# Block 0's residual added after the sums, its squares turned through DRAM, and another pair of PSUM banks, in a decoder trunk with emulated fp32

## The chip, the cores and the metric

The kernel runs on one core of a Trainium2 chip. TensorE does the matmuls and transposes, VectorE and ScalarE the elementwise work, GpSimd (POOL in the profile) and SyncE (SP) issue most DMAs. The metric is the device time of one execution in microseconds. Three runs of the kernel before took 2192.23, 2192.76 and 2198.56 us; the median is 2192.76.

## The reference

One sequence of 256 rows and 2048 features passes through two layers. Layer 0 mixes with gated linear attention, layer 1 with block attention over a shared K/V; each is followed by a gated convolutional FFN, and each part adds its output to the residual h. Cut to what the change touches:

```python
def gla_mixer(x, ...):
    ...
    return o.reshape(B, S, GLA_VAL_DIM).astype(x.dtype) @ w_out

def conv_ffn(x, norm_w, w_up, conv_w, conv_b, w_down):
    h = rms_norm(x, norm_w) @ w_up
    ...
    return (jax.nn.silu(a) * u) @ w_down

def reference(...):
    for layer in range(DEPTH):
        h = h + gla_mixer(...)          # layer 0; moba_mixer in layer 1
        h = h + conv_ffn(h, ffn_norm[layer], ...)
    return h
```

All inputs are float32. Four matrix products end in a residual add: the output projections of the two mixers ("go" and "mo", 2048 by 2048) and the down projections of the two FFNs ("dn0" and "dn1", 5632 by 2048).

## The kernel before

Each float32 operand of a product is split in a high part and the rest (`whi`, `wlo` for weights), and three products of parts are summed in PSUM. For weights, ScalarE casts the high part (L140) and VectorE subtracts it (L141); both run a few steps ahead of TensorE. Weight chunks of 1 MB come by SyncE's queue into `wraw`. One matmul instruction is 128x128 by 128x512.

go, dn0, mo and dn1 all go through `down`. It makes the output in two blocks of 1024 features, b = 0 and 1. A block is a 2 by 2 arrangement of 128x512 pieces: two halves of the rows (t) and two halves of the features (f). Some contraction steps use seven products in place of eight, with sums of operands (`comb`, and weight sums t13 and t24 made by VectorE at L106 to L108); the others are plain. Products carry the numbers 1 to 8. Products 1 and 6, and 5 and 7, share a two-bank tile each and are used by seven-steps only. After the last seven-step they are evacuated: ScalarE copies product 1 into the SBUF tile c0 (L754), VectorE adds the others, giving four tiles c0 to c3 (L755 to L758), and GpSimd issues four accumulating DMAs that add the residual to them (L760). Products 2, 3, 4 and 8 go on. 2 and 3 share a two-bank tile (`low`, "acc" in the trace), 4 and 8 have a bank each ("p"). A block ends with a tail of plain steps, first for f = 0 (products 2 and 4), then for f = 1 (3 and 8); after each, VectorE adds the finished products onto c0 and c2, or c1 and c3 (L769), so it needs the accumulate to have landed, and the piece is done: `done` stores it to DRAM as rows (L782, "rows" in the trace) and ScalarE sums its squares for the next norm (L317). The next block takes new tiles from the same pools, and its first matmuls into a tile wait for the last read of what was there.

The next GEMM needs the sums with features on the partitions. `back` makes that from row pieces: four TensorE transposes (L793) of 128x128, then `make_xw` (ScalarE L253, VectorE L255) scales and splits them into `xw`. `TURNS` says in which block and after which tail step of go and mo the first six of the eight `back` calls come; entry (1, (0, 1)) means block 1, f = 0, step 1. The other two follow the second block.

`turned` holds another way to turn rows into features, used elsewhere in the kernel: VectorE transposes 32x32 squares into `z` (`square`, L384), GpSimd stores z to DRAM (`store`, L387) and loads it back as four strided DMAs (`load`, L393). `through` schedules store, load and the jobs that use the result.

The order on each engine is the order in which the program issues instructions. `after(n, job)` runs a job n weight steps later; `ws.behind()` places what is issued inside it behind the latest weight cast and subtraction. Engines run their queues in order and wait on semaphores; GpSimd's DMAs all stand in one queue of instructions. The four stages lie at about 292 to 383 us (go), 863 to 1110 (dn0), 1381 to 1472 (mo) and 1960 to 2184 (dn1).

Of the kernel before, what the change touches and what calls it, by code (L numbers as in the profile page):

```python
# [9 lines left out]
F32R = mybir.dt.float32r  # L10
I32 = mybir.dt.int32
AF = mybir.ActivationFunctionType
OP = mybir.AluOpType
# [5 lines left out]
S = 256  # L19
KT = D // 128  # L20
NP = KT // 2
# [30 lines left out]
}  # L52


TURNS = ((0, (1, 2)), (0, (1, 2)), (1, (0, 1)), (1, (0, 1)), (1, (1, 2)), (1, (1, 2)))


class WeightStream:
# [99 lines left out]
def trunk(ctx: ExitStack, tc: tile.TileContext, xT, x_tok, cst, msk, w1p, w2a, w_k, w_qa, w_v2, w_v, w_g, w_go,  # L158
          w_up0, w_dn0, w_kk, w_kv, w_mq, w_mo, w_up1, w_dn1, rel, onehot, out):
    nc = tc.nc  # L160
    V, A, T = nc.vector, nc.scalar, nc.tensor
# [11 lines left out]
    def slot(shape, dt, name):  # L173
        return big.tile(shape, dt, name=name, tag="slot")

    def temp(name, shape=(128, 2, S), dt=F32):
        return tmp.tile(list(shape), dt, name=name, tag="temp")

    def bank(name, shape):
        return mis_ps.tile(list(shape), F32, name=name, tag="bank")  # L180
# [5 lines left out]
    ws = WeightStream(tc, raw, parts)  # L186
# [59 lines left out]
    def col(c):  # L246
        return gn[:, c - C_GN:c - C_GN + 1] if C_GN <= c < C_GN + KT else cs[:, c:c + 1]

    def make_xw(p, c, name, src):
        x = slot([128, 2, 2 * S], F32R, name)  # L250
        for i in range(2):
            n = col(c + 2 * p + i)
            hi = A.activation(x[:, i, :S], src[:, i, :], AF.Copy, scale=n)  # L253
            ws.first = ws.first or hi.ins
            V.scalar_tensor_tensor(x[:, i, S:], src[:, i, :], n, x[:, i, :S].bitcast(F32),  # L255
                                   op0=OP.mult, op1=OP.subtract)
        return x

    def spread_sum(ps, sq):
# [9 lines left out]
    def after(steps, job):  # L269
        later.append((cur[0] + steps, job))  # L270
# [31 lines left out]
    def split(dst_hi, dst_lo, src):  # L302
        A.copy(dst_hi, src)
        V.tensor_sub(dst_lo, src, dst_hi.bitcast(F32))

    class Norm:
# [9 lines left out]
        def square(self, t, c, src):  # L316
            A.activation(temp("junk", (128, 512)), src, AF.Square, accum_out=self.ss[:, t, c:c + 1])  # L317
# [27 lines left out]
    nrm = Norm(C_GN, "xw")  # L345
# [9 lines left out]
    xs = rows(nrm.xs)  # L355
# [187 lines left out]
    fresh, square, through = turned("keys", 2)  # L543
# [45 lines left out]
    for g in range(2):  # L589
        z = gemm_tok(xs, 1, lambda ps: evacuated(ps, col16))  # L590
        jobs = []
# [107 lines left out]
                after(7 + 2 * i, lambda J=J, i=i: convolve(2 * J + i, f[J][:, 2 * i:2 * i + 2, :]))  # L699
        then(hid, sums)  # L700

    def down(name, xs, combos, res, done, jobs):

        for b, (order, n_tail) in enumerate(ORDERS[name]):
            new = [k for k, seven in order if seven and k not in combos]
            todo = {i: list(js) for i, js in jobs.get(b, {}).items()}
            for k in new:
                at = next(i for i, (k_, _) in enumerate(order) if k_ == k)
                todo.setdefault(max(at - 2, 0), []).append(lambda k=k: combine_parts(k, xs, combos))
            low = acc_ps.tile([128, 2, 512], F32, name="acc")  # L710
            p = {2: low[:, 0], 3: low[:, 1], 4: bank("p4", (128, 512)), 8: bank("p8", (128, 512))}
            left = dict.fromkeys(range(1, 9), 0)
            for k, seven in order:
                for n in ((1, 5, 7, 6, 4, 3, 2) if seven else (2, 3, 4, 8, 2, 3, 4, 8)):
                    left[n] += 3
            begun = set()

            def prods(*todo):

                w = step()  # L720
                for n, _, _ in todo:
                    if n not in p:
                        two = acc_ps.tile([128, 2, 512], F32, name="acc")
                        p.update({n: two[:, 0], {1: 6, 5: 7}[n]: two[:, 1]})
                for xi, wi in ((0, 0), (1, 0), (0, 1)):
                    for n, x, f in todo:
                        left[n] -= 1
                        T.matmul(p[n], x[xi], w[wi][:, 512 * f:512 * f + 512], start=n not in begun, stop=left[n] == 0)  # L728
                        begun.add(n)

            def part(k, i, t):
                x = xs[k][:, i, 128 * t:]
                return x[:, :128], x[:, S:S + 128]

            def comb(k, f):
                return combos[k][:, f, 0], combos[k][:, f, 1]

            last = max(i for i, (k, seven) in enumerate(order) if seven)
            for i, (k, seven) in enumerate(order[:-n_tail]):
                for job in todo.get(i, ()):  # L740
                    job()
                if seven:
                    prods((1, part(k, 0, 0), 0))
                    prods((3, comb(k, 3), 0), (2, part(k, 1, 0), 1))
                    prods((5, comb(k, 0), 0), (7, comb(k, 2), 1))
                    prods((6, comb(k, 1), 0), (4, part(k, 1, 1), 1))
                else:
                    for a in range(2):
                        prods(*((n, part(k, a, t), f)
                                for n, t, f in ((2, 0, a), (3, 0, 1 - a), (4, 1, a), (8, 1, 1 - a))))  # L750
                if i == last:

                    r = [temp(f"c{n}", (128, 512)) for n in range(4)]
                    A.copy(r[0], p[1])  # L754
                    V.tensor_add(r[1], r[0], p[6])  # L755
                    V.tensor_add(r[2], r[1], p[7])
                    V.tensor_add(r[1], r[1], p[5])
                    V.tensor_add(r[3], r[2], p[5])  # L758
                    for n in (0, 2, 1, 3):
                        nc.gpsimd.dma_start(r[n], res(n // 2, 2 * b + n % 2), accum_op=OP.add)  # L760
            for f, ns in enumerate(((2, 4), (3, 8))):
                for i, (k, _) in enumerate(order[-n_tail:]):
                    for job in todo.get((f, i), ()):
                        job()
                    prods(*((n, part(k, a, t), a) for a in range(2) for t, n in enumerate(ns)))
                if f:
                    ws.prefetch(cur[0])
                for t, n in enumerate(ns):
                    V.tensor_add(r[2 * t + f], r[2 * t + f], p[n])  # L769
                    done(t, 2 * b + f, r[2 * t + f])  # L770

    def scratch(name):
        t = dram.tile([2, 128, D], F32, name=name)
# [37 lines left out]

    def middle(name, xs, combos, res, nrm, keep_row, at, feature_major, parked=None):
        done, back, in_acc, in_bank = onward(nrm, keep_row, parked)
        jobs = {}
        for q, (b, i) in enumerate(at):
            jobs.setdefault(b, {}).setdefault(i, []).append(lambda q=q: back(q, in_acc))
        down(name, xs, combos, res, done, jobs)
        for q in range(len(at), NP):
            after(1 if feature_major else q - 3, lambda q=q: back(q, in_bank))
        after(2 if feature_major else 3, nrm.close)  # L820
        if feature_major:
            after(3, nrm.weave)
# [169 lines left out]
    xs = rows(xkv)  # L992
# [125 lines left out]
```

## Time and profile before

| | before |
|---|---|
| median of three runs | 2192.76 us |
| profiled execution | 2190.33 us |
| its span | 2188.5 us |
| PE busy | 2169.5 us, 99% |
| DVE busy | 1594.4 us, 73% |
| ACT busy | 1283.9 us, 59% |
| POOL busy | 301.9 us, 14% |
| accumulating DMAs (L760), issue to landing | 4.1 to 10.4 us, median 8.8 |
| stores of rows (L782), issue to landing | 2.6 to 7.5 us, median 4.0 |

The span runs from the first to the last instruction; the profiled execution's own time is 1.8 us longer. PE is TensorE's matmuls and PEld its weight loads, which overlap; DVE is VectorE, ACT ScalarE. "p<-whi,hid" is an instruction that writes p and reads whi and hid. In a timeline row the bracket gives how long the engine was idle before it and what ended that.

### The profile page before, as it was taken

How to read it: one execution, taken by the hardware profiler on the slowest of the kernel's cores; microseconds unless marked ns; L12 is line 12 of the kernel's file. 1: busy time of each engine (PE TensorE's matmuls, PEld its weight loads, DVE VectorE, ACT ScalarE, POOL GpSimd, SP SyncE). 2: the span in 40 equal slices, each digit the busy share in tenths (PEclk: the TensorE clock that was granted, in tenths of full speed). 3: DMA queues.
4: the chain of work that ended last, by engine and by line, in shares of the span. 5: the costliest groups of instructions: out<-in, count | busy, mean ns of one | idle time of the engine just before them, and what ended most of it. 6: DMA issues, size and time to landing. Idle time of an engine off the chain costs nothing.

```text
span 2188.5 us, 26953 instructions
## 1 busy us (share of the span) xinstructions
PE 2169.5 (99%) x9693; PEld 1793.0 (82%) x9693; DVE 1594.4 (73%) x2190; ACT 1283.9 (59%) x1856; POOL 301.9 (14%) x448
## 2 busy tenths in 40 slices
PE   9999999999999999999999999999999999999999
PEld 7888887888888888778888888888888888887787
DVE  6655687667676767987867787776777676779886
ACT  6545665556565556555556676555656565656554
POOL 1011111111111111000013242011111111110000
PEclk9999999999999999999999999999999999999999
DMA  8466577677777777566577887676777777775655
GB/s 318 176 231 211 185 245 257 208 239 232 249 244 237 247 238 244 176 234 239 205 262 261 273 277 230 207 234 225 236 249 235 247 238 245 239 245 189 234 206 173
DMA packets 92248, 510.11 MB, mean 233 GB/s; under 512 B 13729, under 2 KB 14769, under 8 KB 42194
## 3 DMA queue, kind: packets, MB, share of 16 engines
q1 hardware_dynamic: 60722, 417.53, 54.4%
q0 software_dynamic: 30816, 90.28, 15.2%
q8 instruction: 76, 1.25, 0.2%
q10 hardware_dynamic: 576, 0.58, 0.1%
q14 instruction: 58, 0.48, 0.1%
HBM read 463.22 MB, written 45.11 MB: 232 GB/s over the span
## 4 chain that ended last, share of the span: by engine, by line
PE 88%; issue 9%; DMA 2%; ACT 1%; DVE 0%; POOL 0%; SPq 0%; DVEq 0%; ACTq 0%; POOLq 0%
PE acc L290 44%; PE acc L293 22%; PE acc L728 12%; PE p L728 7%; DMA c<-rows 1%; DMA w2s<-w2a 0%; PE sT L561 0%; PE o L578 0%; ACT whi L140 0%; PE acc L793 0%; DMA wraw<-w_v 0%; PE s L910 0%; POOL upT L667 0%; DMA gn<-cst 0%; PE z L428 0%
## 5 line engine op out<-in xcount | busy, mean ns | idle before, releaser
L141 DVE TENSOR_TENSOR wlo<-wraw,whi 128x1024 fp32r<-128x1024 f32 (+1 forms) x786 | 930.3, 1191 | 423.3 <-ACT whi L140 402.2
L140 ACT CAST whi<-wraw 128x1024 fp32r<-128x1024 f32 (+1 forms) x786 | 798.8, 1026 | 639.1 <-PE acc L290 417.9
L290 PE MATMUL acc<-whi,xw 128*128 128x512 f32 x3840 | 952.3, 390 | 2.4 <-ACT whi L140 1.7
L290 PEld LDWEIGHTS acc<-whi,xw 128*128 128x128 f32 x3840 | 719.6, 188 | 153.8 <-ACT whi L140 2.8
L293 PE MATMUL acc<-wlo,xw 128*128 128x512 f32 x1920 | 514.3, 389 | 0.0
L293 PEld LDWEIGHTS acc<-wlo,xw 128*128 128x128 f32 x1920 | 360.3, 188 | 74.6
L728 PE MATMUL acc<-whi,hid 128*128 128x512 f32 x572 | 182.3, 390 | 4.5 <-DVE c L769 3.8
L728 PE MATMUL p<-whi,hid 128*128 128x512 f32 x506 | 166.2, 390 | 0.0
L667 POOL DMA_DIRECT2D upT<-turned x176 | 114.3, 656 | 146.4 <-DMA turned<-z 59.3
L140 ACT CAST whi<-t 128x1024 fp32r<-128x1024 f32 x82 | 85.5, 1051 | 77.9 <-PE p L728 42.6
L728 PEld LDWEIGHTS acc<-whi,hid 128*128 128x128 f32 x572 | 106.8, 188 | 28.1 <-DVE c L769 4.6
L290 PE MATMUL acc<-whi,xkv 128*128 128x512 f32 x512 | 128.8, 391 | 0.0
L661 POOL DMA_DIRECT2D turned<-z x44 | 34.2, 776 | 678.1 <-DVE z L657 615.6
L676 ACT ACTIVATE au<-upT,cs 128x256 f32<-128x256 f32 x176 | 96.0, 595 | 45.4 <-DMA upT<-turned 45.3
L728 PE MATMUL acc<-whi,comb 128*128 128x512 f32 x328 | 108.0, 394 | 4.4 <-ACT whi L140 4.3
L728 PEld LDWEIGHTS p<-whi,hid 128*128 128x128 f32 x506 | 94.9, 188 | 19.8
L290 PEld LDWEIGHTS acc<-whi,xkv 128*128 128x128 f32 x512 | 94.6, 188 | 18.6
L141 DVE TENSOR_TENSOR wlo<-t,whi 128x1024 fp32r<-128x1024 f32 x82 | 99.1, 1220 | 4.8 <-ACT whi L140 3.5
L680 DVE SCALAR_TENSOR_TENSOR au<-upT,cs,au 128x255 f32<-128x255 f32 x176 | 77.4, 472 | 33.8 <-ACT au L676 33.7
L728 PE MATMUL acc<-wlo,hid 128*128 128x512 f32 x286 | 94.9, 391 | 1.4 <-DVE wlo L141 1.4
L760 POOL DMA_DIRECT2D c<-rows x24 | 21.2, 1052 | 465.2 <-DVE c L755 453.4
L728 PE MATMUL p<-wlo,hid 128*128 128x512 f32 x253 | 83.6, 389 | 0.0
(251 smaller groups left out, 1951.4 us busy)
## 6 DMA issues: line engine op xcount, KB each, us to landing
wraw<-w_up SPq DMA_DIRECT2D x176, 1024.0 KB, 5.3
wraw<-w_dn SPq DMA_DIRECT2D x88, 1024.0 KB, 4.9
turned<-z POOLq DMA_DIRECT2D x44, 512.0 KB, 3.5
upT<-turned POOLq DMA_DIRECT2D x176, 128.0 KB, 4.8
wraw<-w_g SPq DMA_DIRECT2D x16, 1024.0 KB, 4.9
wraw<-w_go SPq DMA_DIRECT2D x16, 1024.0 KB, 6.2
wraw<-w_mq SPq DMA_DIRECT2D x16, 1024.0 KB, 5.8
wraw<-w_kk SPq DMA_DIRECT2D x16, 1024.0 KB, 5.6
```

The lines of the kernel that those rows point to most:

```text
L140: one = nc.scalar.copy(hi[:, a:b], src[:, a:b])
L141: two = nc.vector.tensor_sub(lo[:, a:b], src[:, a:b], hi[:, a:b].bitcast(F32))
L290: T.matmul(ps[:, t, :], xs(kt)[:, x0 + 128 * t:x0 + 128 * t + 128], hi[:, c:c + 512], start=kt == 0 and x0 == 0, stop=False)
L293: T.matmul(ps[:, t, :], xs(kt)[:, 128 * t:128 * t + 128], lo[:, c:c + 512], start=False, stop=kt == KT - 1)
L661: nc.gpsimd.dma_start(turned[J].rearrange("(a i) r q c -> (i r) a (q c)", a=4), z.rearrange("p (a q) t c -> p a (q t c)", a=4))
L667: nc.gpsimd.dma_start(f[32 * q:32 * q + 32].rearrange("p a (i c) -> p (a i) c", i=4), turned[J][:, :, q, :].rearrange("a r c -> r a c"))
L676: A.activation(au[:, i, :], t[:, i, :], AF.Identity, bias=col(cb + n), scale=col(cw + 2 * 2 * FT + n))
L680: V.scalar_tensor_tensor(au[:, i, 1:], t[:, i, :S - 1], col(cw + 2 * FT + n), au[:, i, 1:], op0=OP.mult, op1=OP.add)
L728: T.matmul(p[n], x[xi], w[wi][:, 512 * f:512 * f + 512], start=n not in begun, stop=left[n] == 0)
L760: nc.gpsimd.dma_start(r[n], res(n // 2, 2 * b + n % 2), accum_op=OP.add)
```

## The change

Three edits, two of them for go and mo only.

In go and mo the first block's accumulating DMAs no longer follow the last seven-step. They are issued one by one after VectorE's add of each finished sum. Four weight steps later `to_dram` stores the rows, sums the squares, and VectorE turns the piece by 32x32 squares into a z tile shared by both row halves. When the second half is in, z goes through DRAM, and eight and nine steps after that `turned_xw` scales the loaded squares on ScalarE (four 128x128 activations each), casts and subtracts (`split`). The four `back` calls of block 0 go away with their transposes, and `TURNS` keeps two entries.

In dn0 and dn1 products 3 and 8 now share the two-bank tile, and 2 and 4 have a bank each. In go and mo the pair stays (2, 3).

```diff
-TURNS = ((0, (1, 2)), (0, (1, 2)), (1, (0, 1)), (1, (0, 1)), (1, (1, 2)), (1, (1, 2)))
+TURNS = ((1, (1, 2)), (1, (1, 2)))
...
+    def turned_xw(p, c, name, f):
+
+        x, w = slot([128, 2, 2 * S], F32R, name), temp("w")
+        for i in range(2):
+            for t in range(2):
+                A.activation(w[:, i, 128 * t:128 * t + 128].rearrange("p (t i c) -> p t i c", t=2, i=2),
+                             f[:, i, :, t::2], AF.Copy, scale=col(c + 2 * p + i))
+        split(x[:, :, :S], x[:, :, S:], w)
+        return x
...
-            p = {2: low[:, 0], 3: low[:, 1], 4: bank("p4", (128, 512)), 8: bank("p8", (128, 512))}
+            pair, single = ((3, 8), (2, 4)) if name.startswith("dn") else ((2, 3), (4, 8))
+            p = {n: low[:, i] for i, n in enumerate(pair)}
+            p.update({n: bank(f"p{n}", (128, 512)) for n in single})
...
-                    for n in (0, 2, 1, 3):
-                        nc.gpsimd.dma_start(r[n], res(n // 2, 2 * b + n % 2), accum_op=OP.add)
+                    if b or not first_done:
+                        for n in (0, 2, 1, 3):
+                            nc.gpsimd.dma_start(r[n], res(n // 2, 2 * b + n % 2), accum_op=OP.add)
...
-                    V.tensor_add(r[2 * t + f], r[2 * t + f], p[n])
-                    done(t, 2 * b + f, r[2 * t + f])
+                    x = r[2 * t + f]
+                    V.tensor_add(x, x, p[n])
+                    if b or not first_done:
+                        done(t, 2 * b + f, x)
+                    else:
+                        nc.gpsimd.dma_start(x, res(t, f), accum_op=OP.add)
+                        after(4, lambda t=t, f=f, x=x: first_done(t, f, x))
...
+        fresh, square, through = turned(f"first_{name}", 2)
+        zs = []
+
+        def to_dram(t, c, x):
+            if t == 0:
+                zs.append(fresh())
+            with ws.behind():
+                done(t, c, x)
+                square(zs[c], x, t)
+            if t:
+                through(c, zs[c], [(8 + i, lambda f, i=i: nrm.xs.append(
+                    turned_xw(2 * c + i, nrm.c, nrm.name, f[:, 2 * i:2 * i + 2]))) for i in range(2)])
+
+        jobs, first = {}, 4 if feature_major else 0
...
-        down(name, xs, combos, res, done, jobs)
+        down(name, xs, combos, res, done, jobs, to_dram if feature_major else None)
```

`Norm.xs`, which `turned_xw` appends to, is the list of `xw` tiles that the next GEMM reads. Line numbers move: L728 becomes L740, L760 becomes L773 (the early accumulates) and L787 (those after the sums), L769 becomes L783, L782 L800, L384, L387 and L393 become L394, L397 and L403, and L317 L327.

TensorE in dn0, before: the end of block 0 and the start of block 1. acc_6975 holds products 2 and 3, p8_6977 product 8, acc_7917 is a tile of the next block.

```order
L728 MATMUL p8_6977<-whi_7811,hid_6943 128x512 [waits Activation_49]
L728 MATMUL p8_6977<-whi_7811,hid_6943 128x512 x3
L728 MATMUL p8_6977<-wlo_7812,hid_6943 128x512 [waits DVE_49]
L728 MATMUL p8_6977<-wlo_7812,hid_6943 128x512
L728 MATMUL p8_6977<-whi_7827,hid_7123 128x512 x4
L728 MATMUL p8_6977<-wlo_7828,hid_7123 128x512 x2
L728 MATMUL acc_7917<-whi_7853,hid_3445 128x512 [waits Activation_49]
L728 MATMUL acc_7917<-whi_7853,hid_3445 128x512 x3
L728 MATMUL acc_6975<-whi_7793,hid_6764 128x512 [waits DVE_49]
L728 MATMUL acc_6975<-whi_7793,hid_6764 128x512 x3
L728 MATMUL acc_6975<-wlo_7794,hid_6764 128x512 x2
```

The same place after the change, where acc_6989 holds products 3 and 8, and p2_7932 and p4_7933 belong to the next block:

```order
L740 MATMUL acc_6989<-wlo_7826,hid_6956 128x512 [waits DVE_49]
L740 MATMUL acc_6989<-wlo_7826,hid_6956 128x512 x3
L740 MATMUL acc_6989<-whi_7841,hid_7137 128x512 x8
L740 MATMUL acc_6989<-wlo_7842,hid_7137 128x512 x4
L740 MATMUL p2_7932<-whi_7867,hid_3458 128x512 [waits DVE_49,Activation_49]
L740 MATMUL acc_7931<-whi_7867,hid_3458 128x512 x2
L740 MATMUL p2_7932<-whi_7867,hid_3458 128x512
L740 MATMUL acc_7931<-whi_7867,hid_3458 128x512 x2
L740 MATMUL p2_7932<-wlo_7868,hid_3458 128x512 [waits DVE_49]
L740 MATMUL acc_7931<-wlo_7868,hid_3458 128x512
L740 MATMUL p4_7933<-whi_7867,hid_3458 128x512 [waits DVE_49]
```

The wait on DVE that stood before product 3's matmuls is no longer there; the first wait on DVE for a tile's last reader now stands at p2 of the next block, and the one at p4 comes after eight matmuls of that block.

GpSimd in go, block 0, before: accumulates of the residual (x_tok) into the c tiles, then stores of the finished rows.

```order
L760 DMA c0_2585<-x_tok 128x512 [waits DMASW1_49,DVE_49]
L760 DMA c1_2586<-x_tok 128x512 [waits DMASW2_49,DVE_49]
L760 DMA c2_2587<-x_tok 128x512 [waits DMASW3_49,DVE_49]
L760 DMA c3_2588<-x_tok 128x512
L782 DMA rows1_2415<-c0_2585 128x512 [waits DMASW5_49,DVE_49]
L782 DMA rows1_2415<-c2_2587 128x512 [waits DMASW6_49,DVE_49]
L782 DMA rows1_2415<-c3_2588 128x512 [waits DMASW7_49,DVE_49]
L782 DMA rows1_2415<-c1_2586 128x512 [waits DMASW0_49,DVE_49]
```

After the change, with the first store of z behind them:

```order
L787 DMA c0_2586<-x_tok 128x512 [waits DMASW1_49,DVE_49,Activation_49]
L787 DMA c2_2588<-x_tok 128x512 [waits DMASW2_49,DVE_49]
L800 DMA rows1_2415<-c0_2586 128x512 [waits DMASW3_49,DMASW1_49]
L787 DMA c3_2589<-x_tok 128x512 [waits DVE_49]
L800 DMA rows1_2415<-c2_2588 128x512 [waits DMASW5_49,DMASW2_49]
L800 DMA rows1_2415<-c3_2589 128x512 [waits DMASW6_49,DMASW4_49]
L787 DMA c1_2587<-x_tok 128x512 [waits DMASW7_49,DVE_49,Activation_49]
L800 DMA rows1_2415<-c1_2587 128x512 [waits DMASW7_49,DMASW0_49]
L397 DMA first_go_2420<-z_2782 128x1024 [waits DVE_49]
```

Each store of rows now waits for the accumulate that fills the tile which it stores, and the accumulates of c3 and c1 stand behind such stores in the queue.

VectorE in go after the change, where block 0's pieces c0 to c3 are turned into the z tiles (L394) between weight subtractions of block 1 (L141):

```order
L394 STREAM_TRANSPOSE z_2782<-c0_2586 128x4x4x32 [waits DMASW1_49]
L394 STREAM_TRANSPOSE z_2782<-c2_2588 128x4x4x32 [waits DMASW2_49]
L141 TENSOR_TENSOR wlo_2866<-t13_2736,whi_2865 128x1024 [waits PE_49]
L141 TENSOR_TENSOR wlo_2809<-t24_2660,whi_2808 128x1024 [waits Activation_49]
L141 TENSOR_TENSOR wlo_2892<-wraw_2722,whi_2891 128x1024 [waits DMAHW3_49,PE_49,Activation_49]
L141 TENSOR_TENSOR wlo_2919<-wraw_2761,whi_2918 128x1024 [waits DMAHW4_49,PE_49,Activation_49]
L394 STREAM_TRANSPOSE z_2845<-c1_2587 128x4x4x32 [waits DMASW7_49]
L394 STREAM_TRANSPOSE z_2845<-c3_2589 128x4x4x32 [waits DMASW4_49]
L141 TENSOR_TENSOR wlo_2855<-wraw_2684,whi_2854 128x1024 [waits Activation_49]
L141 TENSOR_TENSOR wlo_2949<-wraw_2858,whi_2948 128x1024 [waits DMAHW5_49,PE_49,Activation_49]
```

The DMASW waits of the L394 rows are those for the accumulates; the subtractions that follow stand behind them. In the order before, the last row that waits for an accumulate of block 0 is the L769 add of c1, ahead of all the subtractions shown here.

## Rows read from the trace of the kernel before

**Rows 1.** The page: busy time by engine, and the chain by engine.
```profile
PE 2169.5 (99%) x9693; PEld 1793.0 (82%) x9693; DVE 1594.4 (73%) x2190; ACT 1283.9 (59%) x1856; POOL 301.9 (14%) x448
...
PE 88%; issue 9%; DMA 2%; ACT 1%; DVE 0%; POOL 0%; SPq 0%; DVEq 0%; ACTq 0%; POOLq 0%
```
**Rows 2.** TensorE's waits, whole span: total us, times, longest.
```profile
PE acc L728 <- ACT whi L140: 5.1, 4, 2.9
PE acc L728 <- DVE c L769: 3.8, 2, 2.0
...
PE p L728 <- DVE wlo L141: 0.5, 1, 0.5
```
**Rows 3.** The chain of waits at 344 to 346 us: start, us, what.
```profile
344.58 0.45 PE acc L793 x4
```
**Rows 4.** Timeline of TensorE in dn0 between the blocks: start, us, instruction.
```profile
973.53 1.07 PE L728 MATMUL p<-whi,hid 128*128 128x512 f32 x4
...
977.61 1.07 PE L728 MATMUL acc<-whi,hid 128*128 128x512 f32 x4
980.64 1.19 PE L728 MATMUL acc<-whi,hid 128*128 128x512 f32 x4 [1.96 <-DVE c L769]
```
**Rows 5.** Timeline of VectorE at the same place.
```profile
979.89 0.69 DVE L769 TENSOR_TENSOR c<-c,acc 128x512 f32<-128x512 f32 x1 [7.57 <-DMA c<-rows]
980.50 2.35 DVE L141 TENSOR_TENSOR wlo<-wraw,whi 128x1024 fp32r<-128x1024 f32 x2
```
**Rows 6.** Line L760 in dn0's first block (968 to 976 us).
```profile
DMA to landing us min/median/max: 9.0/10.0/10.3
```
**Rows 7.** Timeline of TensorE in dn1 between the blocks.
```profile
2067.32 1.19 PE L728 MATMUL acc<-whi,hid 128*128 128x512 f32 x4 [1.84 <-DVE c L769]
```
**Rows 8.** Timeline of VectorE at the end of dn1.
```profile
2180.58 0.69 DVE L769 TENSOR_TENSOR c<-c,p 128x512 f32<-128x512 f32 x1 [1.86 <-PE p L728]
2184.66 0.69 DVE L769 TENSOR_TENSOR c<-c,acc 128x512 f32<-128x512 f32 x1 [3.39 <-PE acc L728]
```
**Rows 9.** Timeline of ScalarE in go, start of block 1.
```profile
345.01 0.62 ACT L140 CAST whi<-wraw 128x512 fp32r<-128x512 f32 x1 [4.42 <-PE acc L793]
...
347.52 1.04 ACT L140 CAST whi<-t 128x1024 fp32r<-128x1024 f32 x1 [1.52 <-DVE t L106]
348.47 1.04 ACT L140 CAST whi<-wraw 128x1024 fp32r<-128x1024 f32 x1
```
**Rows 10.** Timeline of TensorE in go.
```profile
328.69 0.39 PE L728 MATMUL p<-wlo,go 128*128 128x512 f32 x1
...
349.56 0.80 PE L728 MATMUL acc<-whi,comb 128*128 128x512 f32 x1 [2.93 <-ACT whi L140]
350.16 0.63 PE L728 MATMUL acc<-whi,go 128*128 128x512 f32 x1
350.58 0.63 PE L728 MATMUL acc<-whi,comb 128*128 128x512 f32 x1
...
352.65 0.40 PE L728 MATMUL p<-whi,go 128*128 128x512 f32 x1
```
**Rows 11.** Windows in go: stretch, us, busy by engine, PEclk, DMA share, GB/s.
```profile
340.00:360.00 20.00, 17.07 (x72) 13.67 (x71) 15.61 (x18) 11.70 (x15) 0.00 (x0) 0.91 0.59 221
```
**Rows 12.** Line L760 in go's first block (318 to 330 us).
```profile
DMA to landing us min/median/max: 4.2/6.1/9.0
```
**Rows 13.** Groups of ScalarE by form, L317: busy, mean ns, idle before.
```profile
L317 ACT ACTIVATE junk<-c 128x512 f32<-128x512 f32 x24 | 15.0, 626 | 28.9 <-DVE c L769 24.1 <-PE acc L793 4.8
L317 ACT ACTIVATION_READ_ACCUMULATOR junk<-c 128x1 f32 x24 | 4.5, 186 | 0.0
```
**Rows 14.** Line L387, the stores of turned squares, whole span.
```profile
DMA to landing us min/median/max: 2.6/3.2/10.2
```
**Rows 15.** Line L393, the loads of turned squares, whole span.
```profile
DMA to landing us min/median/max: 2.8/5.0/8.0
```
**Rows 16.** Timeline of TensorE in mo, the step after the f = 0 tail.
```profile
1419.03 1.07 PE L728 MATMUL p<-whi,ox 128*128 128x512 f32 x4
```
**Rows 17.** Line L760 in mo's first block (1405 to 1420 us).
```profile
DMA to landing us min/median/max: 8.4/9.5/10.1
```
**Rows 18.** Line L760 in mo's second block (1440 to 1470 us).
```profile
DMA to landing us min/median/max: 6.5/7.1/8.7
```

More of the change, by code (lines that the diff above doesn't have):

```diff
@@ L700, in ffn, with down @@
         then(hid, sums)
-    def down(name, xs, combos, res, done, jobs):
+    def down(name, xs, combos, res, done, jobs, first_done=None):
         for b, (order, n_tail) in enumerate(ORDERS[name]):
@@ L813, in middle @@
         done, back, in_acc, in_bank = onward(nrm, keep_row, parked)
-        jobs = {}
+        fresh, square, through = turned(f"first_{name}", 2)
[10 more added lines that the diff above has]
+        jobs, first = {}, 4 if feature_major else 0
         for q, (b, i) in enumerate(at):
-            jobs.setdefault(b, {}).setdefault(i, []).append(lambda q=q: back(q, in_acc))
-        down(name, xs, combos, res, done, jobs)
-        for q in range(len(at), NP):
+            jobs.setdefault(b, {}).setdefault(i, []).append(lambda q=q: back(first + q, in_acc))
+        down(name, xs, combos, res, done, jobs, to_dram if feature_major else None)
+        for q in range(first + len(at), NP):
             after(1 if feature_major else q - 3, lambda q=q: back(q, in_bank))
```

## The prediction

> **What bounds the kernel now.** I read the page first, then the waits of TensorE, then single engines around the four places that the diff touches. The page shows TensorE busy for 99% of the span and carrying 88% of the chain of waits [rows 1]. So time can come only from fewer TensorE instructions, or from TensorE's few waits. Those are short: the two largest groups in the list are four waits on ScalarE's casts, 5.1 us together with one of 2.9, and two waits on VectorE's add at L769, 3.8 us [rows 2]. A third thing to look for is new waits: VectorE and ScalarE have spare time, but their queues are in order, and the change puts waits for DMAs into them.
>
> **TensorE's instructions.** Four transposes take 0.45 us on the chain [rows 3], 0.1125 each. `TURNS` shrinks from six entries to two, so four of `back` go in each of go and mo, with four transposes each: 2 x 4 x 4 = 32 transposes, 32 x 0.1125 = **3.6 us less**. Matmuls are the same in number. All 32 stand on TensorE, so this term holds unless a wait eats it.
>
> **Down projections, between the blocks.** In dn0 the f = 0 tail ends and p8's last 18 matmuls begin at 973.53; 4 of the next block's follow at 977.61; then p3 waits until 980.64, 1.96 us [rows 4]. p3 shares a tile with p2, and p2's reader, VectorE's c0 add, began at 979.89 after 7.57 us of waiting for a DMA [rows 5], an accumulate that took 9.0 to 10.3 us to land [rows 6]. Afterwards p3 and p8 share the tile, both are unread, and their 36 matmuls run on: 36 x 0.227 = 8.2 us (the matmul step is that from 973.53 to 977.61: 18 in 4.08), so to 981.7. The new block's first product needs p2, whose add ends at 979.89 + 0.69 = 980.6: in time. Next late is p4: its add stands in VectorE's queue behind three wlo subtractions of about 1.17 each [rows 5], so it ends at 980.6 + 3.5 + 0.7 = 984.8, and TensorE is there after 8 more matmuls, at 983.5. The next block's products wait about 1.2 instead of 1.96: 0.8 less (0 to 1.96). In dn1 the wait is 1.84 [rows 7], and fewer subtractions stand between; I take 1.2 of it as gained (0 to 1.84). Together **2.0 less** (0 to 3.8).
>
> **The end of dn1.** Before, p8's add came at 2180.58 and only p3's, at 2184.66, after the last matmul [rows 8]. Now both adds read the tile that ends last: one add more in series, 2180.58's 0.69, less some overlap: **0.6 more** (0.5 to 0.7). The two stores leave on different queues.
>
> **go, the wait that is there.** ScalarE's cast at 345.01 waited 4.42 us because the L317 and L253 work before it waited for transposes; through VectorE's subtraction and L106 it made the casts of 347.52 and 348.47 late [rows 9]; TensorE stood still for 2.93 us until 349.56, and then issued matmuls 0.42 to 0.43 us apart (350.16, 350.58) instead of 0.23 [rows 10]: the granted clock, 0.91 over 340 to 360 [rows 11], had gone to its lower level, 1.2 GHz instead of 2.4, after the stand-still. Seven matmuls took 3.09 us (349.56 to 352.65) instead of 1.59. The place costs 2.93 + 1.5 = 4.4 us, and with the transposes gone this cause is gone.
>
> **go, the waits that come.** The first block's accumulates now start after its sums are finished, and the POOL order puts stores that wait for a landing between them: c0, c2, store of c0 (waits for c0's landing), c3, stores of c2 and c3 (wait for c3's landing), and only then c1. Three landings stand in series. The f = 0 tail ended at 328.69 + 0.23 [rows 10]; 6 matmuls now stand before its end, so 330.3; the add (0.69) and the issue make c0 start at about 331.3. Two store issues of 0.55 lie between, so c1 lands at 332.4 + 3L. The nearest row for L is go's first block itself: 4.2 to 9.0, median 6.1 [rows 12]. I take 6.1: c1 lands at 350.7.
> Behind it: on ScalarE the squares of c1 and c3 (0.63 each and a read of 0.19 [rows 13]), then four casts 0.95 apart [rows 9]; on VectorE two 32x32 transposes (estimated as other 128x512 operations there, 0.69), then wlo subtractions. Counting TensorE's order at 0.227 per matmul from 330.3, the subtraction behind the two transposes is needed at 353.6, and it ends 7.3 us after c1 lands: no wait while c1 lands before 346.3. At 350.7 TensorE waits 4.4, and a stand-still as long as the present one would again cost about 1.5 at the lower clock: 5.9 against 4.4 now, **1.5 more**. The bounds are L = 4.2 (c1 at 345.0, no wait, 4.4 less) and L = 8.0, short of the largest row since three in series will not all be the longest (356.4: 10.1 + 1.5, so 7.2 more). The store of the squares and its loads (L387 3.2, L393 5.0 median [rows 14, 15]) come after c1, but the 16 activations that read them stand far enough behind it: nothing.
> The Trainium skill, "DMA: Bandwidth & Descriptors", section "Anatomy of one DMA — SWDGE (gpsimd) path", gives such a DMA about 2.0 us plus its bytes over 436 GB/s, so an estimate of 2.6 us for 256 KB. The trace disagrees, with 4.2 at the least in go and 10.3 at the most in dn0 [rows 6, 12]; by the rule three in series would be 7.8 us, and the time would come out as in rival A.
>
> **mo.** Now TensorE loses 0.5 us there, on a subtraction [rows 2]. The f = 0 tail ends at 1419.03 [rows 16], so c0's accumulate would start at about 1420.0. Afterwards POOL's order is c0, c2, the stores of both, c3, c1: two landings in series. L is 8.4 to 10.1, median 9.5 [rows 17]: c2 is issued at 1421.0, lands at 1430.5; c1 is issued at 1432.1 and lands at 1441.6. The same squares and transposes stand before casts that TensorE needs from 1443.5 on; no wait before 1440.2, so 1.4 (0 to 2.6). Then c1's and c3's squares are stored and loaded back: 1441.6 + 0.7 for the transposes, 0.6 + 3.2 for the store, four issues of 0.55 and 5.0 for the loads make 1453.3; eight small activations and two casts (4 us, an estimate) stand before the copy that opens the second block's residual chain, at 1457.4. Its accumulates (6.5 to 8.7 [rows 18]) land about 1466.5, when by its order TensorE wants the banks: 1.5 (0 to 4). Less the 0.5 of now: **2.4 more** (0.5 less to 6 more).
>
> **Sum.** -3.6 - 2.0 + 0.6 + 1.5 + 2.4 = -1.1. The profiled execution took 2190.33 us; 2189.2. The median of the runs shown, 2192.76, lies 2.4 above it, so 2191.6.
>
> **Rivals.** *A, the accumulates land early* (chance 0.30). If L falls to 4.2 in go and 6.5 in mo, because fewer transfers are under way together than when four were issued in a row, no new wait arises: -3.6 - 2.0 + 0.6 - 4.4 - 0.5 = -9.9, so 2182.9. For it: go's shortest landings; ScalarE and VectorE are not full. Against it: every accumulate of dn0 took 9.0 or more [rows 6].
> *B, POOL's series of landings stalls the cast queues* (0.24). With L = 8 in go and 10.1 in mo: -3.6 - 2.0 + 0.6 + 7.2 + 6 = +8.2, so 2201.0. It decides from L of about 7.4 in go; mo's and the second blocks' landings speak for it, go's own median against.
> *C, nothing is gained in the down projections* (within the forecast): p2's or p4's adds still wait for the same DMAs, so the stall only moves to the next block's first products; 2.0 is lost and the time is 2193.6. For it: the landing of c2's accumulate, which I did not move.
> *D, the change does what it says but the order is not what sets it* (within the forecast): waits in the profile are small, so everything is hidden and 3.6 - 0.6 remain: 2189.8.
>
> **How the numbers follow.** The forecast with C and D has 0.46; A 0.30; B 0.24. A measurement of this kernel can't tell less than about 0.3%, 6.6 us, from no change. A lies 9.9 below, so most of it is faster; some of it falls within, and a little of the forecast below -6.6: faster 0.30. B gives slower 0.23. The range must hold 8 in 10: from A's end, 2182, to just past B's, 2201; the forecast's own range is 2186 to 2198.
>
> **What would show it.** Right: no TensorE wait on c L783 between the blocks of dn0 and dn1, or one of about 1 us on the add of p4; two adds after the last matmul; in go a TensorE wait of some 4 us between 350 and 358, with ScalarE's square L327 or VectorE's L394 waiting for DMA c<-x_tok before it; in mo waits of 1 to 2 us near 1445 and 1467. Wrong: no wait in go at all (A), or one of over 8 us followed by a low clock (B); 1.9 us still lost between the blocks of dn0 (C).

## The result: slower, and the profile after

The changed kernel took 2209.76 us (median, 2207.36 to 2215.76), against 2193.9 us (2191.66 to 2198.56) for the kernel before in the same runs: a ratio of 1.0073, with a 95% interval of 1.0062 to 1.0083. The prediction was 2191.6 us, with 2182 to 2201 as its range and 0.23 for slower. The time lies outside.

First the page, against [rows 1]: TensorE's busy time and instructions, then the chain.

```profile
PE 2172.8 (99%) x9661; PEld 1790.2 (81%) x9661; DVE 1596.2 (72%) x2190; ACT 1290.7 (59%) x1880; POOL 312.7 (14%) x468
...
PE 89%; DMA 4%; issue 3%; DVE 2%; ACT 1%; POOL 1%; SPq 0%; DVEq 0%; POOLq 0%; ACTq 0%
```

There are 9661 TensorE records in place of 9693: the 32 transposes are gone. The chain now has 4% DMA in place of 2%. The span is 2205.6 us instead of 2188.5. Here are TensorE's waits over the whole span (total, times, longest), which answer to [rows 2].

```profile
PE acc L740 <- ACT whi L140: 12.1, 6, 7.3
PE p L740 <- ACT whi L140: 4.4, 3, 3.0
PE p L740 <- DVE wlo L141: 3.6, 4, 1.1
PE acc L740 <- DVE wlo L141: 2.3, 8, 0.7
```

The matmuls' waits on the add of the sums (3.8 us) have left the list. Their waits on ScalarE's casts have grown from 5.1 to 16.5 us, and one of them lasts 7.3.

To see where, I split each trace at four instructions of TensorE: the first matmul that reads the operand of go, of dn0 (hid), of mo (ox) and of dn1 (hid). The last column runs to the last matmul. Each stretch holds the stage and what comes between it and the next.

| stretch | before | after | longer by |
|---|---|---|---|
| go, to the start of dn0 | 571.55 | 585.46 | 13.91 |
| dn0, to the start of mo | 517.81 | 517.33 | -0.48 |
| mo, to the start of dn1 | 570.81 | 573.39 | 2.57 |
| dn1, to the last matmul | 232.31 | 232.83 | 0.52 |

So 14 of 17 us are in go's row, and in go itself: the next GEMM's first matmul comes 105.4 us after go's first, where it came 91.4 after it. TensorE's timeline there (start, us, instruction, wait and releaser) answers to [rows 10]; the window below it answers to [rows 11].

```profile
349.87 1.46 PE L740 MATMUL acc<-whi,comb 128*128 128x512 f32 x5 [0.96 <-ACT whi L140]
...
358.10 0.73 PE L740 MATMUL p<-whi,go 128*128 128x512 f32 x2 [2.96 <-ACT whi L140]
...
372.90 0.79 PE L740 MATMUL acc<-whi,comb 128*128 128x512 f32 x1 [7.27 <-ACT whi L140]
373.49 0.63 PE L740 MATMUL p<-whi,go 128*128 128x512 f32 x1
373.92 0.63 PE L740 MATMUL acc<-whi,comb 128*128 128x512 f32 x1
```

```profile
360.00:380.00 20.00, 12.04 (x39) 8.64 (x38) 10.08 (x11) 8.60 (x16) 4.94 (x9) 0.77 0.59 185
```

Of the wait of 2.93 at 349.56, 0.96 is left at 349.87. New are 2.96 and 7.27; after the long one the matmuls come 0.43 us apart (373.49, 373.92) at the lower clock, 1.2 GHz, and the granted clock of the window is 0.77. Go back from 372.90: ScalarE's timeline, then VectorE's.

```profile
355.78 0.63 ACT L327 ACTIVATE junk<-c 128x512 f32<-128x512 f32 x1 [2.83 <-DMA c<-x_tok]
...
370.85 1.04 ACT L140 CAST whi<-wraw 128x1024 fp32r<-128x1024 f32 x1 [10.01 <-DMA wraw<-w_go]
```

```profile
361.06 1.30 DVE L394 STREAM_TRANSPOSE z<-c 128x512 f32<-128x512 f32 x2
362.29 1.18 DVE L141 TENSOR_TENSOR wlo<-wraw,whi 128x1024 fp32r<-128x1024 f32 x1
```

The wait of 2.96 is the one that the prediction was about: c1's accumulate lands, the square L327 of 355.78 starts, the cast behind it is late. The long one is not. ScalarE waited 10.01 us for a weight chunk, `wraw<-w_go`. SyncE issued its load only at 363.49, when the subtraction that ends at 362.29 + 1.18 = 363.47 had read the buffer's old chunk for the last time; the load took 7.3 us:

```profile
DMA to landing us min/median/max: 7.3/7.3/7.3
```

SyncE's load issues after (the row holds three from 352.06, the last at 375.5) and before (five from 337.98):

```profile
352.06 23.72 SPq L96 DMA_DIRECT2D wraw<-w_go  x3
379.42 17.09 SPq L96 DMA_DIRECT2D wraw<-w_up  x4
```

```profile
337.98 19.93 SPq L96 DMA_DIRECT2D wraw<-w_go  x5
360.24 39.95 SPq L96 DMA_DIRECT2D wraw<-w_up  x7
```

Before, the last load of go went out by 357.9; after, at 375.5. GpSimd's accumulates in go's first block (answering to [rows 12]) show that the landings do stand in series:

```profile
338.60 0.89 POOL L787 DMA_DIRECT2D c<-x_tok  x1
340.50 0.58 POOL L800 DMA_DIRECT2D rows<-c  x1 [1.00 <-DMA c<-x_tok]
350.42 0.56 POOL L800 DMA_DIRECT2D rows<-c  x1 [9.35 <-DMA c<-x_tok]
350.97 0.94 POOL L787 DMA_DIRECT2D c<-x_tok  x1
```

```profile
DMA to landing us min/median/max: 4.3/4.9/11.5
```

c3's accumulate went out at 338.60, its store waited until 350.42, and c1's went out at 350.97. That looked like the whole cause. The experiments say that it is not.

### The profile page after: what moved, and what is told of

It is laid out like the page before. It is cut to its first block, busy times and chain, and to the rows that moved or that the text cites. A ratio compares the mean times of both kernels' runs of the same rounds, so it can differ in the third digit from the quotient of the medians.

```text
span 2205.6 us, 26944 instructions
## 1 busy us (share of the span) xinstructions
PE 2172.8 (99%) x9661; PEld 1790.2 (81%) x9661; DVE 1596.2 (72%) x2190; ACT 1290.7 (59%) x1880; POOL 312.7 (14%) x468
## 4 chain that ended last, share of the span: by engine, by line
PE 89%; DMA 4%; issue 3%; DVE 2%; ACT 1%; POOL 1%; SPq 0%; DVEq 0%; POOLq 0%; ACTq 0%
PE acc L300 44%; PE acc L303 22%; PE acc L740 12%; PE p L740 9%; DVE wlo L141 1%; DMA upT<-turned 1%; DMA c<-x_tok 1%; DMA wraw<-w_dn 1%; DMA first_go<-z 1%; ACT whi L140 0%; DMA w2s<-w2a 0%; DMA wraw<-w_mo 0%; PE sT L571 0%; PE o L588 0%; DMA wraw<-w_v 0%
## 5 line engine op out<-in xcount | busy, mean ns | idle before, releaser
L141 DVE TENSOR_TENSOR wlo<-wraw,whi 128x1024 fp32r<-128x1024 f32 (+1 forms) x786 | 929.4, 1190 | 439.9 <-ACT whi L140 418.9
L740 PE MATMUL p<-whi,hid 128*128 128x512 f32 x572 | 204.4, 390 | 1.4 <-ACT whi L140 1.4
L740 PE MATMUL acc<-whi,hid 128*128 128x512 f32 x506 | 167.7, 389 | 0.0
L740 PEld LDWEIGHTS p<-whi,hid 128*128 128x128 f32 x572 | 107.4, 188 | 24.7 <-ACT whi L140 2.7
L740 PE MATMUL acc<-whi,comb 128*128 128x512 f32 x328 | 108.3, 395 | 12.1 <-ACT whi L140 12.1
L740 PEld LDWEIGHTS acc<-whi,hid 128*128 128x128 f32 x506 | 95.0, 188 | 19.7
L740 PE MATMUL p<-wlo,hid 128*128 128x512 f32 x286 | 106.4, 391 | 3.1 <-DVE wlo L141 3.1
L141 DVE TENSOR_TENSOR wlo<-t,whi 128x1024 fp32r<-128x1024 f32 x82 | 98.8, 1215 | 6.0 <-ACT whi L140 4.9
L740 PE MATMUL acc<-wlo,hid 128*128 128x512 f32 x253 | 91.5, 390 | 0.0
L740 PEld LDWEIGHTS acc<-whi,comb 128*128 128x128 f32 x328 | 62.0, 189 | 28.5 <-ACT whi L140 15.8
```

Of the source, the lines that this page charges most:

```text
L141: two = nc.vector.tensor_sub(lo[:, a:b], src[:, a:b], hi[:, a:b].bitcast(F32))
```

## The experiments

Three theories. Theory 1, from the prediction: landings in series hold the cast queues. Theory 2: the added transfers slow the weight loads. Theory 3 came after the first four runs: the change has altered the order in which go's weight chunks are cast, and with three buffers the loads then start late. All ratios are against the kernel before, run beside them.

| run | ratio (95%) | go | mo |
|---|---|---|---|
| changed kernel | 1.0073 (1.0062 to 1.0083) | +13.9 | +2.6 |
| pair_only | 1.0000 (0.9984 to 1.0016) | +2.2 | +0.1 |
| turn_only | 1.0065 (1.0040 to 1.0090) | +12.9 | +5.0 |
| behind | 1.0067 (1.0046 to 1.0089) | +13.4 | +2.0 |
| early | 1.0071 (1.0048 to 1.0093) | +14.2 | +5.2 |
| after_chunks | 1.0047 (1.0032 to 1.0062) | +5.0 | +10.0 |
| early_chunks | 1.0022 (1.0008 to 1.0035) | +5.7 | +2.6 |
| after_raw4 | 0.9981 (0.9966 to 0.9995) | +1.4 | +1.5 |
| behind_raw4 | 0.9978 (0.9968 to 0.9988) | -4.3 | +0.3 |
| early_raw4 | 0.9973 (0.9963 to 0.9983) | -3.4 | -2.3 |
| early_raw4_old | 0.9975 (0.9966 to 0.9984) | -3.9 | -2.3 |
| before_raw4 | 1.0009 (1.0000 to 1.0018) | -0.1 | -0.3 |
| mo_only | 1.0040 (1.0027 to 1.0053) | +5.4 | +4.2 |

go and mo are the stretches of the table above in each run's one profile, less those of before. They vary: in pair_only and mo_only every engine has the same instructions in go, in the same order, as before, and go came out 2.2 and 5.4 us longer; the traces also come from several chips. So differences of up to some 5 us in these two columns carry nothing by themselves.

**pair_only**, the kernel before with

```diff
+            pair, single = ((3, 8), (2, 4)) if name.startswith("dn") else ((2, 3), (4, 8))
```

> The kernel before with the edit of the down projections alone (products 3 and 8 share the tile). By both theories on go and mo nothing happens there. The waits of about 2 us between the blocks of dn0 and dn1 go, but the changed kernel shows new waits of 0.3 to 1.3 us in the second blocks and 1 us more after the last matmul: between 2 us faster and 2 us slower than before, no difference that can be told.

1.0000: the edit of the down projections is worth nothing that can be measured. Between the blocks of dn0 this trace has 0.91 us at p4, where the prediction worked out 1.2, in place of the 1.96 at p3:

```profile
988.27 0.73 PE L730 MATMUL p<-whi,hid 128*128 128x512 f32 x2 [0.91 <-DVE c L771]
```

**turn_only**, the changed kernel with `pair, single = (2, 3), (4, 8)` everywhere.

> The changed kernel with the old pair (2, 3) in dn0 and dn1: the edits of go and mo alone. Both theories: 14 to 18 us slower than before, all of the loss, with some 14 of it in go and 2 to 3 in mo.

As expected: 1.0065. All of the loss that can be measured is in the edits of go and mo.

**behind**, the row stores forced behind all four accumulates:

```diff
-            with ws.behind():
+            with ws.behind(), tc.issue_after(added[0, 1]), tc.issue_after(added[1, 1]):
                 done(t, c, x)
```

> The changed kernel with one thing moved: on GpSimd's queue the four stores of block 0's rows stand behind all four accumulates, so the landings are no longer in series. Theory 1 (landings in series hold ScalarE's squares and VectorE's square transposes, and these hold the subtraction that frees a weight buffer): c1 lands in go by about 350 instead of 355.8, and 6 to 12 of the 16 us lost come back. Theory 2 (the added transfers slow the weight loads themselves): the same transfers run, closer together, and the time stays within 2 us of the changed kernel's.

c1's accumulate went out 10 us earlier, and it had landed by 348.84 at the latest, when its store went out (GpSimd's timeline):

```profile
340.64 0.86 POOL L789 DMA_DIRECT2D c<-x_tok  x1 [4.08 <-DVE c L785]
341.17 1.97 POOL L802 DMA_DIRECT2D rows<-c  x3
348.84 0.54 POOL L802 DMA_DIRECT2D rows<-c  x1 [5.70 <-DMA c<-x_tok]
```

And nothing came back. ScalarE's longest wait in go is still for a weight chunk:

```profile
369.47 1.04 ACT L140 CAST whi<-wraw 128x1024 fp32r<-128x1024 f32 x1 [11.96 <-DMA wraw<-w_go]
```

**early**, the accumulates after the last seven-step as before the change:

```diff
-                    if b or not first_done:
-                        for n in (0, 2, 1, 3):
-                            nc.gpsimd.dma_start(r[n], res(n // 2, 2 * b + n % 2), accum_op=OP.add)
+                    for n in (0, 2, 1, 3):
+                        nc.gpsimd.dma_start(r[n], res(n // 2, 2 * b + n % 2), accum_op=OP.add)
...
-                        nc.gpsimd.dma_start(x, res(t, f), accum_op=OP.add)
```

> The changed kernel with block 0's residual accumulated after the last seven-step as before, so it is on its way while TensorE does the tails; the squares still go through DRAM. Theory 1: no new wait for an accumulate is left, TensorE has 32 transposes less and the old wait of 4.4 us in go is gone: 3 to 9 us faster than before. Theory 2: the store and the loads of the squares still compete with the weight loads: 5 us or more slower than before.

1.0071: theory 1 has fallen as the cause of the loss. No accumulate is late here, and go is as long. ScalarE, then TensorE:

```profile
370.35 1.04 ACT L140 CAST whi<-wraw 128x1024 fp32r<-128x1024 f32 x1 [12.26 <-DMA wraw<-w_go]
```

```profile
372.39 0.79 PE L740 MATMUL acc<-whi,comb 128*128 128x512 f32 x1 [7.83 <-ACT whi L140]
```

Two rows show where the gain went. The wait of 2.96 us at 358.10 had an open load behind the accumulate: with the accumulate out of the way, ScalarE waits there 3.24 us (behind) and 2.32 us (early) for a weight chunk, and TensorE stands still about as long. In behind, then in early:

```profile
357.57 0.50 PE L742 MATMUL acc<-whi,comb 128*128 128x512 f32 x1 [3.12 <-ACT whi L140]
```

```profile
358.14 0.61 PE L740 MATMUL acc<-whi,comb 128*128 128x512 f32 x1 [2.21 <-ACT whi L140]
```

And the load that the long wait hangs on is no better off. It went out some 3 us earlier than in the changed kernel (360.18 and 360.75 instead of 363.49), but took longer to land, 9.2 and 9.5 us instead of 7.3.

Both runs keep the order of the casts in go. That order I had not looked at as a whole. Give the weight chunks a letter in the order of their loads, from the sixth of go (A) to its last (K); L is the first chunk of the next GEMM. Write down ScalarE's casts from the last of chunk F on (t24 or t13 is a cast of a sum; the subtractions on VectorE follow in nearly the same order):

```
before        F t24 G t24 H H I I J J K K L L
after         F t24 H I G J t24 H I K J L K L
after_chunks  F G t24 t13 G H t24 H I I J J K L L K
```

There are three weight buffers, so J is loaded into G's, K into H's, L into I's. Before, five casts stand between the last of G and the first of J: J's load has their time to land. After, the last cast of G stands directly ahead of the first of J, and one cast stands between H's last and K's first: almost the whole landing is open. The VectorE excerpt ahead of the prediction shows it too: wlo_2855 reads wraw_2684 (G) behind the subtractions that read 2722 (H) and 2761 (I), and directly ahead of the one that reads 2858 (J). The load of 363.49 is J's; before the change it went out at 354.17 and took 4.7 us. So of the 7.3 us that stand open now, some 2.6 can be the added transfers' (theory 2); that it stands open at all is the order's.

**after_chunks**, a wide half of a chunk only behind the wide half before it, in go and mo:

```diff
+            held = self.last_read.get(c - 1, ()) if kind == "wide" and n in self.deep else ()
...
+                    for ins in held:
+                        stack.enter_context(self.tc.issue_after(ins))
                     one = nc.scalar.copy(hi[:, a:b], src[:, a:b])
```

> The changed kernel with one rule more on the weight splits of go and mo: a wide half is cast and subtracted only behind the wide half before it, so a weight buffer is read out before the next one is begun, as in the kernel before. Accumulates and POOL's order stay as changed. Theory 3 (the changed order of the weight splits lets go of the three weight buffers late, so SyncE's loads start late and their 5 to 9 us stand open): 8 to 14 of the 16 us lost come back, and the long wait of 7.3 us in go goes. Theory 2 (the added transfers slow the weight loads): no more than 3 us come back. Theory 1 (landings in series) has fallen with the runs 'behind' and 'early'; it would leave this at the changed kernel's time.

It fell short: 1.0047, so some 6 us back. In go the long wait is gone and 9 us have come back, but mo has lost more than 7: the same rule reorders mo too. SyncE issues the last three loads of go within 11 us, where the changed kernel takes 24:

```profile
347.81 10.66 SPq L97 DMA_DIRECT2D wraw<-w_go  x3
```

J's load is out at 354.74, as before the change, with all the added transfers in place. So this run parts theories 2 and 3 in go, and settles nothing for the whole.

**early_chunks**, that rule with the early accumulates.

> The same rule on the weight splits, with block 0's residual accumulated after the last seven-step as before. Theory 3: as good as the kernel before or better, 2186 to 2196. Theory 2: the store and loads of the squares still cost, 2203 or more.

1.0022: in between. Two thirds of the loss are back, and the order that I forced has waits of its own (5.5 us on the add of the sums at the transposes of block 1, go and mo together).

**after_raw4** takes the wait away by another buffer, and leaves the casts interleaved, though not in the same order (from the last F on: F t24 t13 G t13 H G I J t24 H I K L J K L; each chunk now goes into the buffer of the fourth before it):

```diff
-    big = ctx.enter_context(tc.tile_pool(name="big", bufs=35))
-    raw = ctx.enter_context(tc.tile_pool(name="raw", bufs=3))
+    big = ctx.enter_context(tc.tile_pool(name="big", bufs=33))
+    raw = ctx.enter_context(tc.tile_pool(name="raw", bufs=4))
```

> The changed kernel with four weight buffers in place of three, and 33 in place of 35 general slots to make room. The casts in go stay interleaved as in the changed kernel, but a load no longer waits for the buffer that is read out late. Theory 3: the wait of 7.3 us in go goes, and 8 us or more come back, if the two slots less cost nothing elsewhere. Theory 2: one more load under way makes the landings longer; nothing comes back.

0.9981: all of the loss is gone. ScalarE's waits for weights of go, between 300 and 400 us, in the changed kernel and with four buffers:

```profile
ACT whi L140 <- DMA wraw<-w_go: 22.7, 6, 10.0
```

```profile
ACT whi L140 <- DMA wraw<-w_go: 1.5, 1, 1.5
```

SyncE has the last load of go out at 354.25, 21 us earlier than the changed kernel:

```profile
354.25 0.33 SPq L96 DMA_DIRECT2D wraw<-w_go  x1
358.79 20.23 SPq L96 DMA_DIRECT2D wraw<-w_up  x5
```

The transfers are the same. By itself that does not refute theory 2, since a fourth buffer also covers loads that land slowly, and they do: those issued between 330 and 380 us landed in 9.1 us at the median here and in 6.8 before. One of them still shows in this trace. ScalarE waits 4.7 us for a chunk of `w_up`, and TensorE 3.4:

```profile
ACT whi L140 <- DMA wraw<-w_up: 4.7, 1, 4.7
```

```profile
372.70 2.08 PE L740 MATMUL p<-whi,go 128*128 128x512 f32 x4 [3.40 <-ACT whi L140]
```

**before_raw4**, the control: the kernel before with the same two lines.

> The control for the run with four weight buffers: the kernel before with four weight buffers and 33 general slots. Theory 3 (the changed kernel loses in go because its interleaved order lets go of the three buffers late): the order before lets go of them in time, so a fourth gains little here, 0 to 5 us faster than before. Rival (a fourth buffer helps any order, and the run with four says nothing on the order): 10 us or more faster than before.

1.0009: a fourth buffer gives the kernel before nothing. What it mends is what the change brought. The control's order is not quite the old one, since the scheduler's order changed with the buffer (from the last F on: F t24 G t24 H I H J I J K K).

**early_raw4**, both.

> Four weight buffers and 33 slots, block 0's residual accumulated after the last seven-step, squares through DRAM. Theory 3: the open loads go as in the changed kernel with four buffers, and the wait for late accumulates as well: 0 to 6 us faster than the kernel before. If the late accumulates cost nothing in their own right, the same as the changed kernel with four buffers, within 3 us.

0.9973, 6 us faster than before and the lowest ratio of all. TensorE's waits between 300 and 400 us are down to two of about 1 us:

```profile
PE acc L740 <- ACT whi L140: 1.2, 1, 1.2
PE p L740 <- DVE wlo L141: 1.1, 1, 1.1
```

**behind_raw4** and **early_raw4_old** (the latter with the old pair) ask what is left for the landings and for the pair.

> The changed kernel with four weight buffers and GpSimd's row stores behind all four late accumulates. It stands between the changed kernel with four buffers (0.9981) and that with early accumulates as well (0.9973). If the landings in series cost something once buffers are no longer short: 0.1% or more faster than 0.9981. If they cost nothing: 0.998, within 0.1%.

> Four weight buffers, block 0's residual accumulated after the last seven-step, squares through DRAM, and in the down projections the old pair (2, 3). The pair alone measured 1.000 against the kernel before, so if it is worth nothing here either: 0.2 to 0.4% faster than the kernel before, as the run early_raw4. If the pair carries part of that run's gain (up to the two waits of 2 us): 0.1 to 0.2% faster only.

0.9978 and 0.9975 lie within the interval of 0.9973, and with 0.9981 for the series all four overlap. With buffers enough, neither late landings in series nor the pair cost anything that can be told: the middle values lie within 2 us of each other. The intervals do not exclude a few us, and go's stretch, in one profile each, is 5.7 us longer in after_raw4 than in behind_raw4.

**mo_only** edits mo alone, with `TURNS` of before for go.

> The edit of the output projections in mo alone, old pair in the down projections. By the stages of the changed kernel's trace mo is 2.6 us longer: 1 to 4 us slower than before. If go's loss has its counterpart here (late buffers, open loads) it is 8 us or more.

1.0040, some 9 us: the second of the two expectations. The same mechanism shows in mo. With its chunks numbered by their loads (16 is the last, 17 the first of the next GEMM) its casts run "13 14 15 t24 13 14 16 15 17 16 17" in place of "13 13 14 14 15 15 16 16 17 17", and ScalarE waits for a chunk:

```profile
1453.59 1.04 ACT L140 CAST whi<-wraw 128x1024 fp32r<-128x1024 f32 x1 [5.36 <-DMA wraw<-w_mo]
```

mo's stretch accounts for 4 of these 9 us, and go's for 5 in a stage that I did not touch. Whether that part recurs from run to run is open.

## Why the prediction was wrong, point by point

**TensorE's instructions** (-3.6): right in the count, 32 records fewer. What they are worth in time no run shows alone.

**Between the blocks of dn0 and dn1** (-2.0): the mechanism was right, both waits on c are gone, and where p4 waits it waits 0.91. But new waits on wlo stand in the second blocks (1.3 us together in dn0), and all of TensorE's waits in dn0 and dn1 come to 7.1 us in the changed kernel and 8.2 in pair_only, against 7.8 before: 1.0000. The two waits were not fixed amounts either: in turn_only, with the old pair, they are 0.8 each. Rival C, nothing gained there, had the right number for another reason.

**The end of dn1** (+0.6): right in kind. Both adds now follow the last matmul:

```profile
2200.91 1.28 DVE L783 TENSOR_TENSOR c<-c,acc 128x512 f32<-128x512 f32 x2 [5.90 <-PE acc L740]
```

From the last matmul's start to the end of the span it is 5.1 us instead of 4.3, so 0.8 more.

**go, the wait that is there** (4.4 less): most of it went, but the cause was misread, so the size is luck. The step had the cast of 345.01 wait for transposes, as the bracket in [rows 9] has it; those were under way at the same moment (344.58 for 0.45 us). But it needed a weight load, chunk G's, which went out at 337.98 and took 6.9 us to land, so to 344.9:

```profile
DMA to landing us min/median/max: 6.9/6.9/6.9
```

In pair_only, with the same instructions in the same order, the profile names that load for the same cast:

```profile
348.11 0.62 ACT L140 CAST whi<-wraw 128x512 fp32r<-128x512 f32 x1 [4.99 <-DMA wraw<-w_go]
```

ScalarE's work ahead of the cast of 345.01 was done at 340.58. After the change, without these transposes, the same cast waits 6.55 us for the same load, until 347.53, and TensorE still loses the 0.96 us at 349.87; why that is less than 2.93 no run shows. An open load was on the list before the change, and the step took it for something else.

**go, the waits that come** (+5.9, in go +1.5 net, -4.4 to +7.2; go lost 13.9): this step failed. The landings do stand in series, and c1's lands by 355.8 where the step said 350.7; the 2.96 us at 358.10 are its wait, where the step said 4.4. But `behind` and `early` took that away and got nothing back, since the open loads behind it set the pace. The step counted "no wait while c1 lands before 346.3" along VectorE's queue and took it that the weights themselves were there. It never asked of each subtraction whose buffer it frees and where the first reader of the next load stands. That price is 7.3 us of waiting and the low clock after it, and it was a term of neither the sum nor its bounds, though the order was at hand.

**mo** (+2.4): the size in this trace, 2.6, is right and the reason is not, so the match is luck: there is no wait near 1445 or 1467, and the 2.3 us that TensorE waits at 1463.90 follow an open load as in go. In turn_only and early mo came out 5 us longer.

**Rivals.** B came nearest in time (2201.0), and its landings were not the cause. A's premise, no late landing, was made true in `early`, and its time of 2182.9 was missed by 28 us; with four buffers as well (2187.81 in its own runs, 0.9973) some 6 of its 9.9 us appear.

**The Trainium skill's estimate** ("DMA: Bandwidth & Descriptors", "Anatomy of one DMA — SWDGE (gpsimd) path"): accumulates took 4.3 to 11.5 us in go, again not the 2.6 estimated from that page, and the rival that it stood beside, A, came no nearer.

What stays open: which part of the edit made the program's order of casts change (the order follows from the scheduler, and I saw only that the edits of go and mo do it, with early accumulates too); how the 14 us divide between the order and the slower landings (J's load took 4.7 us before, 7.3 after); and the other half of the test, the old kernel with the new order of casts, was not tried.

## What to carry to other kernels

When a change moves instructions, follow the buffers of the stream that feeds the bound engine: for each buffer find the last reader of the old chunk and the first reader of the next, and count what stands between them in the queue. If it is less than one landing, every load is open, and a busy share of 60% on the waiting engine hides it. Here one more buffer, for two of 35 general slots, undid the late release. Test such a buffer in the old kernel too, or the gain can't be put down to the change. And before a wait is booked as one that the change removes, check it against the landing of the load that the same instruction needs.

## What the runs showed of the hardware

A 1 MB weight load took 4.7 to 4.9 us to land before the change (the last three of go, issued from 351.50 on). After it, two such loads issued 1.1 us apart at 338 to 340 us, beside an accumulate of 256 KB that itself took 11.5, took 9.3 and 12.0:

```profile
DMA to landing us min/median/max: 9.3/10.7/12.0
```

And one and the same order of instructions in go gave TensorE waits of 2.93 us [rows 10], 3.86 and 4.46 us in the traces of the kernel before, pair_only and mo_only, with granted clocks of 0.91, 0.91 and 0.83 over 340 to 360. In all three the cast behind it began 0.1 us after chunk G's load had landed, which took 6.9, 7.5 and 7.6 us:

```profile
352.67 0.64 PE L730 MATMUL acc<-whi,comb 128*128 128x512 f32 x1 [3.86 <-ACT whi L140]
```

```profile
354.39 0.79 PE L740 MATMUL acc<-whi,comb 128*128 128x512 f32 x1 [4.46 <-ACT whi L140]
```

A wait that hangs on landings is read from more than one trace.
